# The seven block products of a feed-forward's up projection, in another order

## The chip, the core and the metric

The kernel runs on one core of a Trainium2 chip. The metric is the device time of one execution in microseconds (us); the time given for a kernel is the median of its runs. The kernel before takes 2684.95 us, the median of 3 runs (2684.22 to 2685.54).

The engines are named as the profile names them: PE is TensorE (matmuls), PEld its weight loads, DVE is VectorE, ACT is ScalarE, POOL is GpSimd, SP is SyncE, which only issues DMAs here. ACTq is ScalarE's queue as an issuer of DMAs. L250 is line 250 of the kernel.

## The reference

One decoder layer on x of 1024 rows and 1024 columns, all in float32: a SwiGLU feed-forward, a mixer (attention heads beside a state space scan), a cross-attention on 256 memory rows, and a second feed-forward, each with an RMS norm ahead of it and one behind it. The change touches only the first half of the two feed-forwards.

```python
D_MODEL = 1024; SEQ = 1024; D_FF = 2816
...
def swiglu(h, w_gu, w_down):
    gu = h @ w_gu
    g, u = jnp.split(gu, 2, axis=-1)
    return (jax.nn.silu(g) * u) @ w_down
...
    f = swiglu(rmsnorm(h, ffn1_pre_g[l]), ffn1_w_gu[l], ffn1_w_down[l])
    h = h + 0.5 * rmsnorm(f, ffn1_post_g[l])
...
    f = swiglu(rmsnorm(h, ffn2_pre_g[l]), ffn2_w_gu[l], ffn2_w_down[l])
    h = h + 0.5 * rmsnorm(f, ffn2_post_g[l])
```

## The kernel before, in words

**Numbers.** To keep float32 accuracy on TensorE, each operand is split into a high part (a cast on ScalarE, L248) and a low part (value minus high part, on VectorE, L250), both in the fp32r type. A product takes three matmuls for each slice of 128: high by high, high by low, low by high (mm3, L262). Activations lie transposed in tiles of 128 columns of the model by 512 rows (`XH`, `XL`, in the profile xh, xl), for two halves of the rows (hh = 0 and 1) and eight slices k.

**The up phase** (up_phase, L537) computes silu(g) times u for 22 blocks f of 128 columns of D_FF. For each f there are two weight blocks, G and U, and two halves of the rows: a 2 x 2 block product if the 1024 model columns are halved too. The first three f (PLAIN = 3) are done by plain projections, 96 matmuls each. While they run, the kernel prepares sums and differences of activation blocks, and from f = 3 on each f goes through `seven(f)` (L735), a scheme of seven block products in place of eight, 84 matmuls. B11 and B12 are the tiles of the first four slices of the two halves of rows, B21 and B22 those of the last four (L560). B21 and B12 are, by the time of the first seven, overwritten with differences (`steps` L647, `below` L662, `last` L670); S[1], S[4] and S[5] are sums in tiles of their own.

**The preparation** is driven by a list of events: `at(t, f)` (L675) puts an event at a time of a model clock that counts the matmuls issued so far; when the clock passes t the event's instructions are put into the program. `last(k)`, which writes B12's tiles, comes at the head of the first seven (L839 to L843); in feed-forward 1 `below(k)`, which writes B21's, comes in the last plain projections. Each such combination is one VectorE operation (L641), a cast on ScalarE and a subtraction on VectorE.

**The weights.** `pieces(f)` (L679) makes the seven weight blocks in the order in which the products want them: a sum or difference of quarters on GpSimd (L690) where the block is one, then the split (L248, L250) into a tile of a ring of 6 + NBLK (NBLK is 3 in feed-forward 1, 4 in feed-forward 2). `product` (L728) takes the oldest block and first makes sure that four are on their way (`ahead(4)`, L716). The raw G and U of block f + 1 are loaded when the first piece of block f is made.

**A seven** runs its products in the order B22, B21, S1, S4, B12, S5, B11. Each is 12 matmuls into a PSUM bank of 128 x 512 (`bank`, a ring of seven). Three banks are used twice: B12 accumulates on B22's bank a, S5 on S1's bank c, B11 on B21's bank b. Between the two uses the first content is read: a is copied to t5 by ScalarE (L742), b to d by ScalarE (L746), c is read by VectorE into e = d + c (L752), where d has become d - t5 on GpSimd (L747). Then e += m6 (L756); t1 = silu(a R) (L760); e += a (L762); t0 = silu((d + c) R) (L766, L767); t0 *= b (L770); e -= b (L772); t1 *= e on GpSimd (L773). R is the norm's factor of the row. t0 and t1 are stored by DMAs that ScalarE issues (L570), 4.5 us of the model clock later.

**Order of instructions.** TensorE's order is that of the program text. The other engines' order is set by a tile scheduler from dependences and priorities; the operations in `with self.urgent()` (L95) get a higher priority. The order within an engine is then fixed: an instruction that waits holds up everything behind it on its engine.

**What shares the up phase.** In feed-forward 1, `prepare` (L189) splits other weights of the layer beside the sevens, on ScalarE, VectorE and SP. In feed-forward 2, `act_sums` (L575) loads four stored blocks after every second f (GpSimd issues, L586), combines them on VectorE (L593), and ScalarE issues the stores of the sums (L598); the preparation's loads of x are issued by GpSimd (L625).

After the up phase comes the down projection: `down1` (L849) in feed-forward 1, `down_rows` in feed-forward 2. `down1` writes its operands over the tiles xh and xl.

Of the kernel before, what the change touches and what calls it, by code (L numbers as in the profile page):

```python
# [10 lines left out]
F32 = mybir.dt.float32  # L11
# [3 lines left out]
ALU = mybir.AluOpType  # L15
# [3 lines left out]
P = 128  # L19
S = 1024  # L20
H = 512
# [25 lines left out]
class Kern:  # L47
# [489 lines left out]
    def up_phase(self, sp, sp2, wgu, gpre, act_d, bank, load, plain, sizes, rw=None, begin=None):  # L537

        nc = self.nc
        NFT, NWC, NBLK = sizes  # L540

        fts, es = [self.t(sp, [P, H], F32, "ft", bufs=NFT)], [self.t(sp, [P, H], F32, "e")]

        def sums(dt):
            return {n: [self.t(sp, [P, 2, H], dt, f"S{n}{k}") for k in range(4)] for n in (1, 4, 5)}
# [12 lines left out]
        S = {n: [(x[:, 0], x[:, 1]) for x in v] for n, v in sums(F32R).items()}  # L558
        X = [[(self.XH[hh][k], self.XL[hh][k]) for k in range(KT)] for hh in range(2)]
        B11, B12, B21, B22 = X[0][0:4], X[1][0:4], X[0][4:8], X[1][4:8]  # L560

        def ft():
            return fts.pop() if fts else self.t(sp, [P, H], F32, "ft", bufs=NFT)
# [4 lines left out]
        def store(f, hh, t):  # L568
            o = act_d[f // 2][hh][:, f % 2, :]
            self.later.append((self.clock + 4500, lambda: self.kp(nc.scalar.dma_start(out=o, in_=t))))  # L570
            stored[f // 2] += 1
            if stored[f // 2] == 4 and not begin:
                act_sums(f // 2, self.clock + {0: 32000, 1: 26000}.get(f // 2, 10000))
# [36 lines left out]
        def scaled(t, src, hh):  # L610
            nc.vector.tensor_tensor(out=t, in0=src, in1=self.R[hh], op=ALU.mult)  # L611
            nc.scalar.activation(t, t, AF.Silu)  # L612
# [66 lines left out]
        def pieces(f):  # L679

            G, U = (load(wgu[2 * f + i], [P, KT, P]) for i in range(2))
            yield
            G0, G1, U0, U1 = G[:, 0:4], G[:, 4:8], U[:, 0:4], U[:, 4:8]
            for a, b, op in (
                (G0, G1, ALU.add), (U1, None, None), (G0, U1, ALU.add), (U0, G0, ALU.subtract), (G0, None, None),
                (G1, U1, ALU.subtract), (U0, U1, ALU.add),
            ):
                if b is not None:
                    t = self.t(sp if begin else sp2, [P, 4, P], F32, "wc", bufs=NWC)
                    nc.gpsimd.tensor_tensor(out=t, in0=a, in1=b, op=op)  # L690
                    a = t
                n = self.nblk = (self.nblk + 1) % (6 + NBLK)
                if n < 6:
                    w = self.t(self.wp, [P, 2, 4, P], F32R, ("whi", "wlo")[n % 2], bufs=3)
                else:
                    w = self.t(sp2, [P, 2, 4, P], F32R, "blk", bufs=NBLK)
                self.split(w[:, 0], w[:, 1], a)
                yield w

        def blocks():  # L700
            cur = pieces(PLAIN)
            next(cur)
            yield
            for f in range(PLAIN, NFF):
                nxt = None
                for i in range(7):
                    w = next(cur)
                    if i == 0 and f + 1 < NFF:
                        nxt = pieces(f + 1)
                        next(nxt)  # L710
                    yield w
                cur = nxt
# [11 lines left out]
        def block():  # L724
            ahead(4)
            return ready.pop(0)

        def product(ps, x, more=False):  # L728

            w = block()  # L730
            self.more = more
            self.mm3(ps, [(w[:, 0, k, :], w[:, 1, k, :], *x[k]) for k in range(4)], not more, True)
            self.more = False

        def seven(f):  # L735


            t5, d = (self.t(self.tp, [P, H], F32, f"sq{i}") for i in range(2))
            a = bank()
            product(a, B22)  # L740
            with self.urgent():
                nc.scalar.copy(t5, a)  # L742
            b = bank()
            product(b, B21)
            with self.urgent():
                nc.scalar.copy(d, b)  # L746
            nc.gpsimd.tensor_tensor(out=d, in0=d, in1=t5, op=ALU.subtract)  # L747
            c = bank()
            product(c, S[1])
            e = es.pop() if es else self.t(sp, [P, H], F32, "e")  # L750
            with self.urgent():
                nc.vector.tensor_tensor(out=e, in0=d, in1=c, op=ALU.add)  # L752
            m6 = bank()
            product(m6, S[4])
            with self.urgent():
                nc.vector.tensor_tensor(out=e, in0=e, in1=m6, op=ALU.add)  # L756
            product(a, B12, True)
            t1 = ft()
            with self.urgent():
                scaled(t1, a, 1)  # L760
            with self.urgent():
                nc.vector.tensor_tensor(out=e, in0=e, in1=a, op=ALU.add)  # L762
            product(c, S[5], True)
            t0 = ft()
            with self.urgent():
                nc.vector.tensor_tensor(out=t0, in0=d, in1=c, op=ALU.add)  # L766
            scaled(t0, t0, 0)  # L767
            product(b, B11, True)
            with self.urgent():
                nc.vector.tensor_tensor(out=t0, in0=t0, in1=b, op=ALU.mult)  # L770
            with self.urgent():
                nc.vector.tensor_tensor(out=e, in0=e, in1=b, op=ALU.subtract)  # L772
            nc.gpsimd.tensor_tensor(out=t1, in0=t1, in1=e, op=ALU.mult)  # L773
            store(f, 0, t0)
            store(f, 1, t1)
# [3 lines left out]
        t0, dt = (T0 + 12000, 7000) if begin else (T0 + 24000, 6500)  # L779
# [64 lines left out]
        for f in range(PLAIN, NFF):  # L844
            seven(f)
# [1492 lines left out]
```

## Time and profile before

| | before |
|---|---|
| median of 3 runs | 2684.95 us (2684.22 to 2685.54) |
| the profiled execution | 2688.81 us |
| its span | 2687.0 us |
| granted TensorE clock, mean over the span | 0.993 |
| idle time of PE by the page | 2687.0 - 2626.5 = 60.5 us |
| bytes moved | 477.75 MB, 178 GB/s in the mean |

How the rows of the prediction are read. The page's line of engines gives busy time, its share of the span and the number of instructions. The rows of the windows view begin with a stretch of the span and its length; then follows the busy time, with the number of instructions, of PE, PEld, DVE, ACT and POOL, then the mean granted TensorE clock, the busy share of the DMA engines, and GB/s. A row of the timeline gives the start of an instruction, its duration, the engine, the line, the operation, what it writes and reads with shapes, and xN if N alike ran on without a break; a bracket at the end is idle time of the engine just ahead of it and what ended that. Names of buffers are the program's: mm is a PSUM bank of the ring's first three, dn one of the other four, wraw and raw raw weights, wc a combined weight block, whi, wlo and blk split weight blocks, sq the tiles t5 and d, ft t0 and t1.

The groups that the change touches, in the page's numbers: GpSimd's weight combinations (L690) take 1433 to 1505 ns each where they run from raw tiles (114 of them, 167.4 us), the splits' casts (L248) 913 ns for a whole G or U of 128 x 1024, and the silu of a result (L612) 631 ns.

### The profile page before, as it was taken

The page shows a single profiled execution, that of the slowest core. Times are in us where ns is not written, and L with a number is a line of the kernel's source. Part 1 is how long each engine was busy: PE and PEld are TensorE (multiplying, and loading weights), DVE is VectorE, ACT ScalarE, POOL GpSimd, SP SyncE. Part 2 cuts the span into 40 slices and gives each one's busy share as a digit, 9 for nine tenths or more (in the row PEclk, how much of TensorE's full clock was granted, in tenths as well). Part 3 has the DMA queues.
Part 4 walks back from the last instruction along what each step waited for, and adds up shares of the span by engine and source line. Part 5 has one row for each costly group of instructions (what it writes and reads, how often), then busy time and mean ns, then how long its engine had stood idle before and what let it go on. Part 6 is the DMA issues. An engine that isn't in the chain of part 4 may idle for free.

```text
span 2687.0 us, 36694 instructions
## 1 busy us (share of the span) xinstructions
PE 2626.5 (98%) x12970; PEld 2179.5 (81%) x12970; DVE 1886.6 (70%) x2907; ACT 1272.3 (47%) x2263; POOL 605.0 (23%) x712
## 2 busy tenths in 40 slices
PE   9899999999999999999999999999999899999998
PEld 7788888888777778888888897887877788887787
DVE  7788887467568775677777877775557966566777
ACT  7444444445235563555555554354545333333553
POOL 2555553000100000111111110101013655552000
PEclk9999999999999999999999999999999999999999
DMA  5578888984532215544444465444357443447554
GB/s 211 186 266 283 277 287 274 341 290 156 205 125 79 79 67 189 142 107 108 119 119 124 152 193 206 173 141 149 110 181 270 161 162 132 147 140 277 166 169 149
DMA packets 204009, 477.75 MB, mean 178 GB/s; under 512 B 25009, under 2 KB 33585, under 8 KB 203825
## 3 DMA queue, kind: packets, MB, share of 16 engines
q1 hardware_dynamic: 157888, 366.59, 40.9%
q0 software_dynamic: 25344, 71.32, 8.8%
q10 hardware_dynamic: 20592, 37.50, 3.7%
q8 instruction: 102, 1.67, 0.3%
q14 instruction: 83, 0.67, 0.1%
HBM read 322.48 MB, written 131.86 MB: 169 GB/s over the span
## 4 chain that ended last, share of the span: by engine, by line
PE 80%; DMA 7%; DVE 7%; issue 3%; ACT 2%; POOL 0%; SPq 0%; DVEq 0%; ACTq 0%; POOLq 0%
PE mm L137 44%; PE dn L137 28%; PE z L137 2%; PE tr L140 2%; PE y L137 1%; PE ms L137 1%; PE ms L140 1%; DMA wraw<-act 1%; PE seg L137 1%; DMA oraw<-mix 1%; DVE wlo L250 1%; DMA wraw<-in_w_dn 1%; DMA dwlo<-bl 0%; DMA raw<-act 0%; PE st L137 0%
## 5 line engine op out<-in xcount | busy, mean ns | idle before, releaser
L137 PE MATMUL mm<-xh,whi 128*128 128x512 f32 x1364 | 537.2, 404 | 7.1 <-ACT xh L248 2.7
L137 PE MATMUL mm<-xh,wlo 128*128 128x512 f32 x1316 | 504.9, 393 | 0.6 <-ACT xh L248 0.6
L137 PE MATMUL mm<-xl,whi 128*128 128x512 f32 (+1 forms) x1258 | 490.5, 390 | 3.6 <-DVE xl L250 3.2
L137 PEld LDWEIGHTS mm<-xh,whi 128*128 128x128 f32 x1364 | 257.4, 189 | 52.8 <-issue 3.8
L137 PEld LDWEIGHTS mm<-xh,wlo 128*128 128x128 f32 x1316 | 247.9, 188 | 55.0 <-ACT xh L248 1.0
L137 PEld LDWEIGHTS mm<-xl,whi 128*128 128x128 f32 x1258 | 238.2, 189 | 39.1 <-DVE xl L250 4.6
L1734 DVE TENSOR_TENSOR_SCAN nb<-nb,begin 128x128 f32<-128x128 f32 (+7 forms) x128 | 171.8, 1353 | 57.9 <-ACT nb L1730 57.5
L1730 ACT ACTIVATE nb<-z,scale 128x128 f32<-128x128 f32 (+2 forms) x192 | 107.8, 580 | 80.6 <-PE z L137 80.3
L248 ACT CAST whi<-wraw 128x1024 fp32r<-128x1024 f32 (+1 forms) x102 | 93.1, 913 | 101.4 <-PE mm L137 63.5
L137 PE MATMUL dn<-xh,wlo 128*128 128x512 f32 x396 | 136.2, 391 | 1.5 <-DMA wlo<-dwlo 1.5
L250 DVE TENSOR_TENSOR wlo<-wraw,whi 128x1024 fp32r<-128x1024 f32 x70 | 85.4, 1221 | 55.4 <-ACT whi L248 55.0
L137 PE MATMUL dn<-xh,whi 128*128 128x512 f32 x356 | 122.8, 390 | 0.0
L1751 POOL DMA_DIRECT2D mix<-sq x64 | 52.8, 825 | 227.9 <-DVE sq L1749 166.8
L690 POOL TENSOR_TENSOR wc<-raw,wraw 128x512 f32<-128x512 f32 x56 | 84.3, 1505 | 74.6 <-issue 26.4
L690 POOL TENSOR_TENSOR wc<-wraw,raw 128x512 f32<-128x512 f32 x58 | 83.1, 1433 | 71.5 <-DVE blk L250 17.0
L612 ACT ACTIVATE ft<-ft 128x512 f32<-128x512 f32 x88 | 55.4, 631 | 76.3 <-DVE ft L611 75.8
L773 POOL TENSOR_TENSOR ft<-ft,e 128x512 f32<-128x512 f32 x38 | 62.2, 1637 | 129.0 <-DVE e L772 102.7
L250 DVE TENSOR_TENSOR atl<-tr,ath 128x512 fp32r<-128x512 f32 (+1 forms) x108 | 67.9, 632 | 32.1 <-ACT ath L248 31.6
L137 PE MATMUL dn<-xh,blk 128*128 128x512 f32 x280 | 90.3, 389 | 0.0
L137 PEld LDWEIGHTS dn<-xh,wlo 128*128 128x128 f32 x396 | 74.6, 188 | 17.7 <-DMA wlo<-dwlo 2.0
L137 PE MATMUL mm<-ath,v 128*128 128x256 f32 x320 | 86.0, 291 | 0.2 <-ACT ath L248 0.2
L250 DVE TENSOR_TENSOR whi<-wc,whi 128x512 fp32r<-128x512 f32 x80 | 64.7, 810 | 30.6 <-ACT whi L248 24.2
(542 smaller groups left out, 6614.8 us busy)
## 6 DMA issues: line engine op xcount, KB each, us to landing
whi<-dwhi SPq DMA_DIRECT2D x78, 512.0 KB, 3.3
wlo<-dwlo SPq DMA_DIRECT2D x78, 512.0 KB, 4.3
wraw<-in_w_gu SPq DMA_DIRECT2D x44, 512.0 KB, 4.1
act<-ft ACTq DMA_DIRECT2D x88, 256.0 KB, 2.5
raw<-in_w_gu SPq DMA_DIRECT2D x38, 512.0 KB, 4.4
h<-F POOLq DMA_DIRECT2D x40, 256.0 KB, 3.0
xl<-h POOLq DMA_DIRECT2D x40, 256.0 KB, 5.7
dwhi<-acc SPq DMA_DIRECT2D x39, 256.0 KB, 5.1
```

The costliest lines, as they stand in the source:

```text
L137: self._pe(self.nc.tensor.matmul(out, lhsT, rhs, start=start, stop=stop, skip_group_check=self.more), cost)
L140: self._pe(self.nc.tensor.transpose(out, src, self.ident if ident is None else ident), 109.0)
L248: self.kp(self.nc.scalar.copy(hi, src))
L250: self.nc.vector.tensor_tensor(out=lo, in0=src, in1=hi.bitcast(F32), op=ALU.subtract)
L612: nc.scalar.activation(t, t, AF.Silu)
L690: nc.gpsimd.tensor_tensor(out=t, in0=a, in1=b, op=op)
L773: nc.gpsimd.tensor_tensor(out=t1, in0=t1, in1=e, op=ALU.mult)
L1730: nc.scalar.activation(nb[:, s0:s1], z[:, 0:n], AF.Sigmoid, scale=sc[:, i : i + 1])
L1734: nc.vector.tensor_tensor_scan(out=nb[:, 0:Wd][:, ::-1], data0=nb[:, 0:Wd][:, ::-1], data1=begin[:, S - Wd : S][:, ::-1], initial=0.0, op0 ...
L1751: nc.gpsimd.dma_start(out=self.mix_d[p][a * 64 : a * 64 + 64, csl], in_=o, accum_op=ALU.add)
```

## The change

The seven products of `seven(f)` run in the order B22, S1, S4, B21, S5, B11, B12. The weight pieces (L684) are made in the order that goes with it. The banks' pairs are the same: S5 on S1's, B11 on B21's, B12 on B22's. Since d does not exist yet when S1 is done, S1's bank is copied to e by ScalarE, S4's is added to e by VectorE, and d is added to e by VectorE after S5. The last product of a seven is now B12, whose bank gives t1 by scaling and silu; B11 is the last but one. In the changed kernel's own line numbers S1's copy to e is L747, e += m6 L751, B21's copy to d L755, GpSimd's d - t5 L756, t0 = d + c L760, e += d L763, B11's t0 *= b L766 and e -= b L768, B12's e += a L774 and the GpSimd product L775; behind `seven` all lines are higher by two.

```diff
--- before.py
+++ after.py
@@ -682,8 +682,8 @@
             yield
             G0, G1, U0, U1 = G[:, 0:4], G[:, 4:8], U[:, 0:4], U[:, 4:8]
             for a, b, op in (
-                (G0, G1, ALU.add), (U1, None, None), (G0, U1, ALU.add), (U0, G0, ALU.subtract), (G0, None, None),
-                (G1, U1, ALU.subtract), (U0, U1, ALU.add),
+                (G0, G1, ALU.add), (G0, U1, ALU.add), (U0, G0, ALU.subtract), (U1, None, None), (G1, U1, ALU.subtract),
+                (U0, U1, ALU.add), (G0, None, None),
             ):
                 if b is not None:
                     t = self.t(sp if begin else sp2, [P, 4, P], F32, "wc", bufs=NWC)
@@ -740,36 +740,38 @@
             product(a, B22)
             with self.urgent():
                 nc.scalar.copy(t5, a)
+            c = bank()
+            product(c, S[1])
+            e = es.pop() if es else self.t(sp, [P, H], F32, "e")
+            with self.urgent():
+                nc.scalar.copy(e, c)
+            m6 = bank()
+            product(m6, S[4])
+            with self.urgent():
+                nc.vector.tensor_tensor(out=e, in0=e, in1=m6, op=ALU.add)
             b = bank()
             product(b, B21)
             with self.urgent():
                 nc.scalar.copy(d, b)
             nc.gpsimd.tensor_tensor(out=d, in0=d, in1=t5, op=ALU.subtract)
-            c = bank()
-            product(c, S[1])
-            e = es.pop() if es else self.t(sp, [P, H], F32, "e")
+            product(c, S[5], True)
+            t0 = ft()
             with self.urgent():
-                nc.vector.tensor_tensor(out=e, in0=d, in1=c, op=ALU.add)
-            m6 = bank()
-            product(m6, S[4])
+                nc.vector.tensor_tensor(out=t0, in0=d, in1=c, op=ALU.add)
+            scaled(t0, t0, 0)
             with self.urgent():
-                nc.vector.tensor_tensor(out=e, in0=e, in1=m6, op=ALU.add)
+                nc.vector.tensor_tensor(out=e, in0=e, in1=d, op=ALU.add)
+            product(b, B11, True)
+            with self.urgent():
+                nc.vector.tensor_tensor(out=t0, in0=t0, in1=b, op=ALU.mult)
+            with self.urgent():
+                nc.vector.tensor_tensor(out=e, in0=e, in1=b, op=ALU.subtract)
             product(a, B12, True)
             t1 = ft()
             with self.urgent():
                 scaled(t1, a, 1)
             with self.urgent():
                 nc.vector.tensor_tensor(out=e, in0=e, in1=a, op=ALU.add)
-            product(c, S[5], True)
-            t0 = ft()
-            with self.urgent():
-                nc.vector.tensor_tensor(out=t0, in0=d, in1=c, op=ALU.add)
-            scaled(t0, t0, 0)
-            product(b, B11, True)
-            with self.urgent():
-                nc.vector.tensor_tensor(out=t0, in0=t0, in1=b, op=ALU.mult)
-            with self.urgent():
-                nc.vector.tensor_tensor(out=e, in0=e, in1=b, op=ALU.subtract)
             nc.gpsimd.tensor_tensor(out=t1, in0=t1, in1=e, op=ALU.mult)
             store(f, 0, t0)
             store(f, 1, t1)
```

## The prediction

> **What bounds the kernel now.** I read the page first, then the busy time by windows, TensorE's rows in order of time where the windows show gaps, and last the other engines' rows around those gaps.
>
> ```profile
> span 2687.0 us, 36694 instructions
> PE 2626.5 (98%) x12970; PEld 2179.5 (81%) x12970; DVE 1886.6 (70%) x2907; ACT 1272.3 (47%) x2263; POOL 605.0 (23%) x712
> 80.00:105.00 25.00, 18.15 (x65) 13.21 (x64) 23.55 (x25) 15.08 (x26) 16.81 (x17) 0.88 0.48 171
> 105.00:200.00 95.00, 95.00 (x412) 78.41 (x411) 75.62 (x96) 43.20 (x76) 57.06 (x36) 0.98 0.72 244
> 2068.00:2122.00 54.00, 43.72 (x175) 33.50 (x174) 47.11 (x52) 24.40 (x42) 35.87 (x32) 0.95 0.45 151
> 2122.00:2300.00 178.00, 178.00 (x778) 147.20 (x777) 123.77 (x169) 58.94 (x102) 101.04 (x87) 0.99 0.44 153
> 302.45 19.04 PE dn L137 x84
> ```
>
> TensorE is busy 98%. Inside the seven-product loops it is busy 95.00 of 95.00 us and 178.00 of 178.00 us: there the order of products can save nothing, it can only break something. One seven (84 matmuls) takes 19.04 us, a product 2.72 us, a matmul 2.72 / 12 = 0.227 us. TensorE is idle at the head of each feed-forward's loop: 18.15 of 25 us with VectorE busy 23.55, and 43.72 of 54 with VectorE busy 47.11. TensorE's rows there:
>
> ```profile
> 80.15 0.39 PE L137 MATMUL mm<-xh,whi 128*128 128x512 f32 x1
> ...
> 87.55 0.50 PE L137 MATMUL mm<-xl,wlo 128*128 128x512 f32 x1 [2.93 <-DVE xl L250]
> ...
> 101.22 0.50 PE L137 MATMUL mm<-xh,whi 128*128 128x512 f32 x1 [2.10 <-ACT xh L248]
> 102.96 0.80 PE L137 MATMUL mm<-xl,whi 128*128 128x512 f32 x1 [1.24 <-DVE xl L250]
> ...
> 103.98 5.30 PE L137 MATMUL dn<-S,wlo 128*128 128x512 f32 x12
> ...
> 111.89 0.39 PE L137 MATMUL dn<-xh,blk 128*128 128x512 f32 x1
> ```
>
> ```profile
> 2074.37 0.50 PE L137 MATMUL mm<-xh,whi 128*128 128x512 f32 x1 [0.45 <-ACT whi L248]
> ...
> 2082.62 0.73 PE L137 MATMUL dn<-S,whi 128*128 128x512 f32 x2 [1.19 <-ACT whi L248]
> ...
> 2094.68 0.50 PE L137 MATMUL mm<-xl,whi 128*128 128x512 f32 x1 [1.13 <-DVE xl L250]
> 2102.33 0.39 PE L137 MATMUL dn<-xh,blk 128*128 128x512 f32 x1
> ...
> 2120.48 5.49 PE L137 MATMUL mm<-S,whi 128*128 128x512 f32 x12 [4.39 <-DVE e L752]
> ...
> 2128.81 0.39 PE L137 MATMUL mm<-xh,whi 128*128 128x512 f32 x1
> ```
>
> The first seven of feed-forward 1 runs from 80.15 to 111.89, 31.74 us: 12.7 lost, waiting for B21's and B12's operands (xh, xl) and then running S5 at half pace. Feed-forward 2's first seven (2074.37 to 2102.33) loses 8.9; its second (to 2128.81) loses 7.4, because S5 accumulates into S1's bank and VectorE reads that bank late (e L752). So 29.0 us, 1.1%, is all there is to win.
>
> **The change part by part.** *Matmuls* are the same 84 per seven; banks and their ring of seven are the same.
>
> *Later use of B21 and B12.* B21 goes from second to fourth, B12 from fifth to seventh: 5.44 us more for each.
>
> ```profile
> 88.84 0.69 DVE L250 TENSOR_TENSOR xl<-bh,xh 128x512 fp32r<-128x512 f32 x1 [0.68 <-ACT xh L248]
> ...
> 101.20 1.71 DVE L250 TENSOR_TENSOR xl<-bh,xh 128x512 fp32r<-128x512 f32 x1
> ```
>
> In feed-forward 1, B21's last operand is ready at 89.53. TensorE would ask for it at 80.15 + 3 x 2.72 + 9 x 0.227 = 90.35: no wait. B12's last comes at 102.91; asked for at 98.5 if nothing else waits, later if something does.
>
> *A new reader, on ScalarE.* S1's bank was read by VectorE (e = d + c, L752). Now ScalarE copies it to e; S5 is fifth, so it must wait for that copy. In the built program's order this copy stands where the copy of B21's bank (L746) stood, behind a cast of B12's operand and a block's cast:
>
> ```profile
> 94.67 0.62 ACT L248 CAST xh<-bh 128x512 fp32r<-128x512 f32 x1 [0.30 <-DVE bh L641]
> 95.20 0.62 ACT L248 CAST blk<-wc 128x512 fp32r<-128x512 f32 x1
> 95.72 0.58 ACT L746 COPY sq<-mm 128x512 f32<-128x512 f32 x1
> ```
>
> So it ends near 96.3, held by VectorE's chain, not by TensorE. TensorE reaches S5 at 80.15 + 4 x 2.72 = 91.03: a wait of 5.3 us. After the idle time at 98.7 to 103 and before 2120.48, twelve matmuls took 5.30 and 5.49 us, so I take S5 at half pace: 96.3 + 5.3 = 101.6. B11 then needs ScalarE's copy of B21's bank (L755 of the changed kernel), which stands behind the casts of two blocks of the next seven; the second needs a GpSimd combination that in the trace starts at 100.70:
>
> ```profile
> 100.70 1.65 POOL L690 TENSOR_TENSOR wc<-wraw,raw 128x512 f32<-128x512 f32 x1 [1.23 <-DVE blk L250]
> ```
>
> Taking about 99.5 for it there (the GpSimd subtraction ahead of it moves away), copy done 102.4, then B11 and B12: 102.4 + 5.44 = 107.9 against 111.89. **Gain 4.0**; bounds 0 (the copies 4 us later) and 12.7.
>
> The Trainium skill ("TensorE: Matmul & The Clock Gate", Part 1) says the clock halves only after an idle window of about 3.4 us. The trace agrees at 2120.48 (4.39 us idle) but at 101.22 and 102.96 single gaps of 2.10 and 1.24 us, one matmul between them, sufficed. By the page's rule taken gap by gap, the 2.5 us wait that I expect below ahead of B11 would stay at full pace, and the sum would be 10.4 instead of 8.4.
>
> *Feed-forward 2, first seven.* Block 1 is now a combination, and GpSimd makes it ahead of eight DMA issues:
>
> ```profile
> 2073.62 4.25 POOL L625 DMA_DIRECT2D blk<-h  x8
> 2081.46 0.58 ACT L746 COPY sq<-mm 128x512 f32<-128x512 f32 x1 [2.13 <-PE mm L137]
> 2081.94 0.62 ACT L248 CAST whi<-wc 128x512 fp32r<-128x512 f32 x1
> ```
>
> Those loads start 1.3 us later. Block 2's cast stands behind ScalarE's copy of the second product's bank, as it does now (81.46, then 81.94, and TensorE idle 1.19 + 0.66): S4 loses about 2.0. B12's waits go, but block 5's split stands behind VectorE's new e + d, which waits for GpSimd's d - t5, which waits for B21's copy: I put B11's wait at 2.5 to 3.8 us, half pace after it 2 us. Lost: 1.5 (first product, unchanged) + 2.0 + 3.0 + 2.0 = 8.5 against 8.9. **Gain 0.4**; bounds 0 less 3 and 7.4.
>
> *Feed-forward 2, second seven.* VectorE's late read is gone; ScalarE's copy stands behind two DMA issues of the activations' sums (L598) that wait for VectorE:
>
> ```profile
> 2112.41 0.33 ACTq L598 DMA_DIRECT2D xs<-xl  x1
> 2114.71 0.33 ACTq L598 DMA_DIRECT2D xs<-xl  x1
> 2114.00 0.68 DVE L593 TENSOR_TENSOR xl<-cb,cb 128x512 f32<-128x512 f32 x1
> 2119.75 0.68 DVE L752 TENSOR_TENSOR e<-sq,mm 128x512 f32<-128x512 f32 x1
> ```
>
> By these rows the copy is possible at 2115.0, 4.7 us before VectorE's read today; S5 would be asked for near 2102 + 10.9 = 2112.9. That costs a wait of 0 to 2.2 plus part of the half pace; I take 3.4 lost of today's 7.4. **Gain 4.0**; bounds 0 and 7.4.
>
> *Steady sevens.* ScalarE gets 38 copies of 0.58 us: 22 us beside its 47%; cover is there. The cover of B21's bank falls from four products between its copy and B11 to one, 2.72 us. SP: G's raw tile is released by piece 6 instead of 4, so the load two sevens ahead starts some 5 us later, of a whole seven's cover: 0. Ends: feed-forward 1's down projection writes its operands over B12's tiles, free 5.44 us later; they are wanted 4 steps of 5.44 us into that stage, and are cast now at 454.31, where the seven ends at 111.89 + 18 x 19.04 = 454.6: 0. Feed-forward 2's end goes through scale, silu and one GpSimd product instead of two VectorE operations and the same product: 0.1. If those covers fail it costs what rival 3 says.
>
> **Sum:** 4.0 + 0.4 + 4.0 = 8.4. The profiled execution (2688.81 around a span of 2687.0) lies 3.9 above the median; against itself it would go to 2680.4, and the median to 2684.95 - 8.4 = 2676.6.
>
> **Rivals.** (1) *The copies come in time*: VectorE, relieved of waiting for products, runs ahead and none of the three stalls remains but the first product's 1.5: 29.0 - 1.5 = 27.5 less, 2657.5. For it: 2119.75 is late only by VectorE's backlog. Against: VectorE busy 23.55 of 25.
>
> (2) *The stall only changes its name*: S5 and B11 wait as long as B12 did; 2684.95, between 2680 and 2690. For it: VectorE, the engine that is late, loses no instruction.
>
> (3) *Slower: the one-product cover fails in every other seven of feed-forward 2.* There ScalarE's copy of B21's bank stands behind three DMA issues that wait for VectorE's sums, and these for a load:
>
> ```profile
> 2230.04 0.55 POOL L586 DMA_DIRECT2D dg<-act  x1 [0.81 <-DMA act<-ft]
> 2232.84 1.46 DVE L593 TENSOR_TENSOR xl<-cb,cb 128x512 f32<-128x512 f32 x2 [3.02 <-DMA cb<-act]
> 2228.66 0.56 POOL L586 DMA_DIRECT2D cb<-act  x1
> 2347.83 1.29 DVE L593 TENSOR_TENSOR xl<-cb,cb 128x512 f32<-128x512 f32 x2 [3.93 <-DMA cb<-act]
> ```
>
> The load from 2228.66 was used at 2232.84, 4.2 us; so dg is there at 2234.2, two sums 2235.5, the issues and the copy 2236.6. That seven starts at 2128.81 + 5 x 19.04 = 2224.0 and asks for B11 at 2237.6: 1.0 us to spare. At 2347.83 the load came 0.75 us later in its seven. From 1 us of lateness on it costs; 2.2 us in each of 8 sevens is 18 us: 2676.6 + 18 = 2694.6.
>
> **How the numbers follow.** Forecast (gain 5.4 to 16): 0.50. Rival 1 (more than 16): 0.12. Rival 2: 0.25. Rival 3: 0.13. A measurement of this kernel tells about 0.2%, 5.4 us, from no change. So faster 0.62, same 0.25, slower 0.13. The likeliest is 2676.6. The range goes from part of rival 1 (2664) to the end of rival 2 (2690); rival 3 and the best of rival 1 lie outside. The forecast's own range is 2669 to 2680.
>
> **What would show it.** Right: in feed-forward 1's first seven no wait on xl or xh in B21, a wait of about 5 us ahead of S5 (dn or mm<-S) put down to ScalarE's new copy, and the second seven starting near 107.9; the wait on e in feed-forward 2's second seven gone or below 2.5 us; TensorE without gaps in 2122 to 2440. Wrong: gaps ahead of B11 in every other seven (rival 3), or the heads' lost time unchanged (rival 2), or S5 started without a wait (rival 1).

## The result and the profile after

The changed kernel takes 2698.06 us (median of 7 runs, 2695.74 to 2699.64), the kernel before 2685.54 (7 runs, 2684.22 to 2692.53): a ratio of 1.0042, 95% interval 1.0032 to 1.0052. It is slower by about 0.4%, where 2676.6 was forecast. The profiled execution took 2699.64 around a span of 2697.9.

The first lines of the page and two stretches of the windows view (columns as before) of the kernel after:

```profile
span 2697.9 us, 36779 instructions
PE 2627.8 (97%) x12970; PEld 2178.1 (81%) x12970; DVE 1885.7 (70%) x2907; ACT 1287.7 (48%) x2301; POOL 605.1 (22%) x712
140.00:460.00 320.00, 317.00 (x1386) 260.65 (x1385) 259.77 (x336) 155.99 (x283) 165.43 (x108) 0.99 0.81 274
2130.00:2470.00 340.00, 331.34 (x1445) 271.30 (x1444) 216.84 (x308) 115.87 (x204) 179.09 (x146) 0.99 0.44 155
```

TensorE's busy time is 1.3 us more and its idle time 70.1 us instead of 60.5: of the 10.9 us by which the span is longer, 9.6 are idle. And idle time lies where there was none: in the steady sevens, 3.0 us of 320 and 8.7 of 340. TensorE's own rows of the kernel after name what it waited for (not all of them are shown):

```profile
96.38 5.41 PE L137 MATMUL mm<-S,whi 128*128 128x512 f32 x12 [5.47 <-ACT e L747]
102.36 0.50 PE L137 MATMUL dn<-xh,wlo 128*128 128x512 f32 x1 [0.57 <-ACT sq L755]
...
220.97 0.75 PE L137 MATMUL mm<-xh,whi 128*128 128x512 f32 x1 [2.17 <-ACT sq L755]
...
2126.59 0.50 PE L137 MATMUL mm<-xh,whi 128*128 128x512 f32 x1 [2.62 <-ACT sq L755]
...
2147.41 0.50 PE L137 MATMUL dn<-xh,blk 128*128 128x512 f32 x1 [1.46 <-ACT sq L755]
2169.88 0.66 PE L137 MATMUL mm<-xh,blk 128*128 128x512 f32 x1 [3.11 <-ACT sq L755]
...
2327.72 0.50 PE L137 MATMUL dn<-xh,whi 128*128 128x512 f32 x1 [1.86 <-ACT sq L755]
```

The first row is the head that was forecast: S5 waits for S1's copy and then runs at half pace. All the other rows shown are one thing: B11, the first matmul into B21's bank after ScalarE's copy L755. In feed-forward 2 they come in the second and third seven, and from the fourth on in every other. S1's copy (L747) makes three shorter waits that are not shown: 0.26 and 0.49 us in feed-forward 1's second and seventh seven, 1.64 in feed-forward 2's second.

To compare kernels I cut each trace at the sevens. A seven starts 2.72 us (new order) or 5.44 us (old order) ahead of its first matmul on S1; feed-forward 2's first is taken from its first matmul (2074.37 in before, 2079.50 in after), since it has a gap within the first product. A is the start of feed-forward 1's second seven, B the time lost in the 17 from there to the start of its last (over 17 x 19.04), C the length of feed-forward 2's first two sevens, D the time lost in the 16 from its third to the start of its last (over 16 x 19.04), E the rest, so that A + 323.68 + B + C + 304.64 + D + E is the span.

| kernel (run) | A | B | C | D | E | span | median |
|---|---|---|---|---|---|---|---|
| before | 111.89 | 0.0 | 54.4 | 0.0 | 1892.4 | 2687.0 | 2685.5 |
| before, second trace (e0) | 110.48 | 0.0 | 53.3 | 1.0 | 1890.1 | 2683.2 | |
| after | 107.93 | 6.6 | 52.7 | 13.0 | 1889.4 | 2697.9 | 2698.1 |
| d on VectorE (e1) | 108.35 | 0.2 | 53.8 | 6.6 | 1886.1 | 2683.3 | 2687.1 |
| B12, then B11 (e2) | 106.14 | 4.1 | 49.6 | 4.1 | 1889.9 | 2682.1 | 2684.7 |
| sums stored by SyncE (e3) | 106.15 | 6.6 | 48.3 | 14.8 | 1889.1 | 2693.2 | 2694.9 |
| old order, S1 copied by ScalarE (e4) | 107.58 | 6.9 | 51.8 | 1.3 | 1903.1 | 2699.0 | 2700.5 |
| the same by VectorE (e4 vector) | 109.99 | 5.4 | 53.2 | 2.7 | 1896.9 | 2696.6 | 2700.2 |
| first two sevens new (e5) | 107.31 | 1.7 | 51.5 | 5.8 | 1889.8 | 2684.5 | 2687.7 |
| e1 and sums 5 us later (e6) | 108.45 | 0.2 | 55.0 | 1.3 | 1887.6 | 2680.8 | 2685.7 |
| e2's order in the heads alone (e8) | 106.09 | 1.6 | 48.5 | 8.9 | 1889.8 | 2683.1 | 2687.9 |
| e1 and e2 together (e7) | 105.55 | 1.6 | 48.8 | 0.1 | 1888.4 | 2672.7 | 2674.3 |
| e7, S1 copied by VectorE | 107.25 | 1.5 | 48.3 | 4.1 | 1885.7 | 2675.2 | 2683.4 |
| old order, d on VectorE (e9) | 109.51 | 0.0 | 51.5 | 0.1 | 1893.8 | 2683.3 | 2682.8 |

Runs of one kernel spread by 1 to 15 us here, and one trace is one execution: the two traces of before differ by 1.0 to 2.3 us in A, C, D and E each. Differences of that size are not read. The ratios below are to the kernel before, run beside each kernel (medians 2685.66 to 2686.5).

### The profile page after: what moved, and what is told of

Read it like the earlier page. It is cut to its first block, busy times and chain, and to the rows that moved or that the text cites. A ratio compares the mean times of both kernels' runs of the same rounds, so it can differ in the third digit from the quotient of the medians.

```text
span 2697.9 us, 36779 instructions
## 1 busy us (share of the span) xinstructions
PE 2627.8 (97%) x12970; PEld 2178.1 (81%) x12970; DVE 1885.7 (70%) x2907; ACT 1287.7 (48%) x2301; POOL 605.1 (22%) x712
## 4 chain that ended last, share of the span: by engine, by line
PE 69%; DVE 7%; DMA 5%; issue 4%; ACT 2%; POOL 1%; SPq 0%; ACTq 0%; DVEq 0%; POOLq 0%
PE mm L137 38%; PE dn L137 22%; PE z L137 2%; PE tr L140 2%; PE y L137 1%; PE ms L137 1%; PE ms L140 1%; PE seg L137 1%; DMA act<-ft 1%; DMA raw<-act 1%; DVE whi L250 1%; DVE wlo L250 1%; POOL wc L690 1%; DMA oraw<-mix 0%; PE st L137 0%
## 5 line engine op out<-in xcount | busy, mean ns | idle before, releaser
L248 ACT CAST ath<-tr 128x512 fp32r<-128x512 f32 (+1 forms) x108 | 58.9, 546 | 57.4 <-PE tr L140 52.5
L137 PE MATMUL mm<-atl,v 128*128 128x256 f32 x320 | 83.0, 282 | 0.7 <-DVE atl L250 0.7
```

The source lines that it names most:

```text
L137: self._pe(self.nc.tensor.matmul(out, lhsT, rhs, start=start, stop=stop, skip_group_check=self.more), cost)
L248: self.kp(self.nc.scalar.copy(hi, src))
```

## Where the copy was late

One such chain, feed-forward 2's gap at 2327.72, from the rows of GpSimd, VectorE and ScalarE (kernel after). The seven at hand starts at 2312.10:

```profile
2304.51 0.59 ACT L755 COPY sq<-mm 128x512 f32<-128x512 f32 x1
```

```profile
2304.97 1.28 POOL L690 TENSOR_TENSOR wc<-wraw,raw 128x512 f32<-128x512 f32 x1 [0.33 <-DVE wlo L250]
2306.95 1.60 POOL L690 TENSOR_TENSOR wc<-raw,wraw 128x512 f32<-128x512 f32 x1 [0.70 <-DVE whi L250]
2308.52 1.28 POOL L756 TENSOR_TENSOR sq<-sq,sq 128x512 f32<-128x512 f32 x1
```

```profile
2309.83 0.69 DVE L763 TENSOR_TENSOR e<-e,sq 128x512 f32<-128x512 f32 x1 [2.43 <-POOL sq L756]
...
2315.43 0.68 DVE L774 TENSOR_TENSOR e<-e,dn 128x512 f32<-128x512 f32 x1
```

```profile
2316.86 1.30 POOL L775 TENSOR_TENSOR ft<-ft,e 128x512 f32<-128x512 f32 x1
2320.73 0.56 POOL L586 DMA_DIRECT2D dg<-act  x1 [1.32 <-DMA act<-ft]
```

```profile
2325.39 1.29 DVE L593 TENSOR_TENSOR cb<-cb,dg 128x512 f32<-128x512 f32 x2 [3.14 <-issue]
```

```profile
2318.19 0.33 ACTq L570 DMA_DIRECT2D act<-ft  x1
...
2326.11 0.93 ACTq L598 DMA_DIRECT2D xs<-cb  x2
2327.08 0.59 ACT L755 COPY sq<-dn 128x512 f32<-128x512 f32 x1 [5.02 <-DVE cb L593]
```

In the seven before, B21's bank was copied by 2305.10, but GpSimd makes d = d - t5 only behind two weight combinations; VectorE stands 2.43 us for it, and t0's and t1's operations stand behind that. So t1 is finished late, ScalarE issues its store at 2318.19, the load of dg, which waits for that store, is issued at 2320.73, 8.63 us into the seven, VectorE's sums (L593) wait for dg until 2325.39 (this row names no releaser; the row of the same operation in e1, below, names the load), ScalarE's stores of the sums (L598) wait for VectorE, and L755 stands behind them. B11 asked for the bank at 2312.10 + 5 x 2.72 = 2325.7.

The later this load, the longer the seven. In feed-forward 2's even sevens from the fourth to the fourteenth, dg is issued 9.95, 6.84, 7.03, 6.72, 8.63 and 7.60 us into the seven, and the seven is 5.0, 0.5, 0.9, 0.4, 2.2 and 1.1 us too long (in the sixteenth and eighteenth 6.8 into it, and 0.4 and 0.7 too long); in the trace of before the same six loads are issued at 7.07, 6.54, 6.03, 5.84, 5.87 and 5.96.

In feed-forward 1's longest such gap (220.97) L755 stands behind a cast of the background split (L209), whose target is still being stored:

```profile
219.81 0.62 ACT L209 CAST rpost<-braw 128x512 fp32r<-128x512 f32 x1 [1.54 <-DMA dwhi<-rpost]
220.33 0.58 ACT L755 COPY sq<-mm 128x512 f32<-128x512 f32 x1
```

## The experiments

**e1: d made by VectorE.**

```diff
-            with self.urgent():
-                nc.scalar.copy(d, b)
-            nc.gpsimd.tensor_tensor(out=d, in0=d, in1=t5, op=ALU.subtract)
+            with self.urgent():
+                nc.vector.tensor_tensor(out=d, in0=b, in1=t5, op=ALU.subtract)
```

> Change after, with one part replaced: d = b - t5 is made by one VectorE operation that reads B21's bank, in place of ScalarE's copy (L755) and GpSimd's subtraction (L756). Theory Q (ScalarE's queue: the copy L755 stands in order behind instructions that wait, the casts of the background split L209 in feed-forward 1 and the issues L598 of the sums in feed-forward 2, and S5's 2.72 us is all its cover): feed-forward 1's 6.6 us of lost time after its first seven go, of feed-forward 2's 13.0 at least half, since VectorE's sums still wait for the same load: 2698.1 - 6.6 - 6.5 to 13 = 2678 to 2685. Theory D (the root is d itself: GpSimd makes it late, VectorE stands waiting for it, so t0, t1, t1's store and the load that the sums wait for all come late): the same in feed-forward 1, and in feed-forward 2 the load of dg is issued about 3 us earlier in its seven and nearly all of the 13.0 goes: 2678 to 2680. Rival L (not the queue, but the 38 more copies on ScalarE and the weight blocks' other order cost the time): the copies of S1's bank and the blocks' order are still there, so 2692 to 2698.

Measured: 2687.1, ratio to before 1.0005 (0.9996 to 1.0014). B fell from 6.6 to 0.2, D from 13.0 to 6.6: all of feed-forward 1, half of feed-forward 2. The load of dg is issued 5.8 us into its seven (2149.71, the seven from 2143.92) instead of 6.7 to 10: theory D is right in that. But VectorE still stands for that load, and now d itself stands behind it:

```profile
2154.70 1.29 DVE L593 TENSOR_TENSOR cb<-cb,dg 128x512 f32<-128x512 f32 x2 [3.25 <-DMA dg<-act]
...
2157.72 0.68 DVE L755 TENSOR_TENSOR sq<-mm,sq 128x512 f32<-128x512 f32 x1
```

```profile
2158.45 0.50 PE L137 MATMUL mm<-xh,blk 128*128 128x512 f32 x1 [0.78 <-DVE sq L755]
```

So theory Q's half stands too. Rival L (the extra copies themselves cost; the next expectation has its price) falls for the steady sevens: the copies of S1 and the blocks' order were all there. The median lies 2 us above Q's range, further above D's. Since e1 takes a copy off ScalarE and an operation off GpSimd at once, it does not say which of the two made feed-forward 1's loss.

**e2: B12 ahead of B11**, the last two weight pieces exchanged with them: two products of cover for B21's copy instead of one.

```diff
-                (U0, U1, ALU.add), (G0, None, None),
+                (G0, None, None), (U0, U1, ALU.add),
...
-            product(b, B11, True)
...
             product(a, B12, True)
...
+            product(b, B11, True)
```

> Change after, with its last two products exchanged (S5, B12, B11, and the last two weight pieces with them): B21's copy has two products, 5.44 us, before B11 asks for the bank. Theory Q: the longest wait was 3.1 us, so the steady gaps go: 2698.1 - 6.6 - 13.0 = 2678.5; in feed-forward 1's first seven B12 is asked for at 101.8, about 1 us before its last operand is there, so 2679.5; 2677 to 2683. Theory D: the copy's wait is covered all the same, as in Q, but t0 and e still come late and so do the store and the load: the wait on ScalarE may grow beyond 3.1, 2680 to 2686. Rival L: as many copies as before, 2695 to 2700.

Measured: 2684.66, ratio 1.0000 (0.9990 to 1.0009). From feed-forward 1's third seven and feed-forward 2's fifth on no seven is longer than 19.04. What stays lies near the heads: S1's copy in feed-forward 1's second seven (all of B), and B21's copy, above all, in feed-forward 2's fourth:

```profile
119.54 4.41 PE L137 MATMUL dn<-S,whi 128*128 128x512 f32 x12 [2.36 <-ACT e L747]
...
2162.16 0.50 PE L137 MATMUL mm<-xh,blk 128*128 128x512 f32 x1 [2.36 <-ACT sq L755]
```

The extra copies alone, then, do not make the steady loss: e2 has them all. That the second product of cover is the cure is shown only in part, because e2 moves the dates too (ScalarE's rows in e2, one of feed-forward 1 and one of feed-forward 2):

```profile
216.47 0.59 ACT L755 COPY sq<-mm 128x512 f32<-128x512 f32 x1 [0.73 <-PE mm L137]
...
2235.91 0.59 ACT L755 COPY sq<-dn 128x512 f32<-128x512 f32 x1 [3.70 <-DVE cb L593]
```

In feed-forward 1 the copy now waits for its own product alone and ends 11.7 us into each seven from the third on (after: up to 16.7), where even the changed kernel would ask for the bank only at 5 x 2.72 = 13.6. It is no longer late there, and the runs do not say which part of the new order did that. In feed-forward 2 the load of dg is issued 5.8 us into five of the eight even sevens (after: 6.7 to 10), but the copy still stands behind VectorE's sums, and from the sixth seven on ends up to 14.3 us in: there the second product hides up to 0.7 us.

The total is 1.7 us above theory Q's range, by the waits near the heads, and inside theory D's; but D's late load is there mainly in one seven, feed-forward 2's fourth (11.7 us into it).

**e3: the sums' stores (L598) issued by SyncE.**

```diff
-                self.kp(nc.scalar.dma_start(out=xs_d[n, j], in_=x.pop(n)))
+                self.kp(nc.sync.dma_start(out=xs_d[n, j], in_=x.pop(n)))
```

> Change after, with the stores of the activations' sums in feed-forward 2 (L598) issued by SyncE instead of ScalarE: nothing on ScalarE ahead of L755 waits for VectorE's sums any more. Theory Q: the gaps ahead of B11 in feed-forward 2 go (up to 13.0 us), feed-forward 1 keeps its 6.6: 2698.1 - 11 to 13 = 2685 to 2687. Theory D: the lateness of d is untouched, L755 comes in time and TensorE does not see it: the same 2685 to 2687, with the load of dg as late in its seven as now (about 9 us); it differs from Q only in what it leaves in the rows. Rival L: 2695 to 2700.

Measured: 2694.94, ratio 1.0038 (1.0026 to 1.0051). Both theories' 2685 to 2687 missed, and the time lies at the edge of rival L's range: D did not fall, it is 14.8. Feed-forward 1 kept its 6.6, and dg is issued 8.8 to 11.2 us into its seven, as theory D had it. In feed-forward 2's steady sevens the wait at B11 is gone and has moved to S5, which waits for S1's copy; ahead of that ScalarE stands at the store of t1:

```profile
2177.90 0.50 PE L137 MATMUL dn<-xh,wlo 128*128 128x512 f32 x1 [1.34 <-DVE e L774]
2182.01 3.06 PE L137 MATMUL dn<-S,whi 128*128 128x512 f32 x12 [1.10 <-ACT e L747]
```

```profile
2179.94 0.33 ACTq L570 DMA_DIRECT2D act<-ft  x1
2180.36 0.59 ACT L742 COPY sq<-dn 128x512 f32<-128x512 f32 x1 [2.45 <-POOL ft L775]
...
2181.37 0.59 ACT L747 COPY e<-dn 128x512 f32<-128x512 f32 x1
```

The seven started at 2168.24, so t1's store comes 11.7 us into it; VectorE's part of the seven before (L774, for which B21's bank waits too) is as late. Taking one waiting instruction out of ScalarE's queue left the lateness, and the next one held the queue.

**e4: old order, S1's bank copied by ScalarE and d added to e after S5** (one part of the change alone), **and the same with the copy on VectorE.**

```diff
-                nc.vector.tensor_tensor(out=e, in0=d, in1=c, op=ALU.add)
+                nc.scalar.copy(e, c)        # second run: nc.vector.tensor_copy(e, c)
...
             scaled(t0, t0, 0)
+            with self.urgent():
+                nc.vector.tensor_tensor(out=e, in0=e, in1=d, op=ALU.add)
```

> Kernel before in its old order of products and weight blocks, with one part of the change alone: S1's bank is copied to e by ScalarE and d is added to e by VectorE after S5, 38 more ScalarE copies of 0.58 us. Theories Q and D: the copy of B21's bank keeps its four products of cover, S1's copy has two, nothing in the steady sevens is late: 2685.5 less up to 4 (the wait of 4.4 us on e in feed-forward 2's second seven goes), 2681 to 2687. Rival L: the copies cost as in the change, 2691 to 2698.

> As the run with the old order and S1's bank copied to e (2700.5), with the copy on VectorE instead of ScalarE: as many instructions more, none on ScalarE. If ScalarE's queue made the 15 us (the copy behind casts of the background split that wait for stores), they go: 2685.7 plus or minus 3. If the extra operations themselves or the later end of e (d added after S5) made them: 2693 to 2701.

Measured: 2700.5, ratio 1.0056 (1.0043 to 1.0069), and 2700.19, ratio 1.0052 (1.0039 to 1.0065). Theories Q and D failed, and rival L came nearest (2.5 us above its range): this small part alone costs 15 us in the old order. It is not that S1's copy stands in ScalarE's queue, since the copy on VectorE costs as much; whether the extra operations or the later end of e make it, the two runs do not separate. It is lost in feed-forward 1 (B 6.9 and 5.4) and behind it (E), where the down projection waits for ScalarE's copies of its own banks (L945): 7.4 us in e4, 4.1 in the second run, 0.5 in before. The longest of e4's:

```profile
480.01 0.50 PE L137 MATMUL mm<-xh,whi 128*128 128x512 f32 x1 [2.66 <-ACT F L945]
```

The windows view of 140 to 430, first before, then e4 (the fifth number is VectorE's busy time):

```profile
140.00:430.00 290.00, 290.00 (x1281) 240.15 (x1280) 238.33 (x302) 135.22 (x238) 170.91 (x107) 1.00 0.82 277
```

```profile
140.00:430.00 290.00, 287.47 (x1251) 232.92 (x1250) 256.73 (x294) 133.86 (x245) 170.77 (x104) 1.00 0.80 270
```

VectorE works 18 us more with 8 operations fewer: 0.87 us each instead of 0.79. In e1 it is 225.02 us with 318, 0.71 each, and GpSimd has 138.69 us instead of 170.91:

```profile
140.00:430.00 290.00, 290.00 (x1281) 240.11 (x1280) 225.02 (x318) 135.51 (x240) 138.69 (x90) 1.00 0.84 280
```

In feed-forward 1 VectorE had little slack, and what it has depends on how its operations fall beside GpSimd's. That e4's loss comes from this is argued from these rows and not shown; no run took GpSimd's operations away in e4.

**e5: the new order in the first two sevens of each feed-forward alone; e8: e2's order in feed-forward 1's first and feed-forward 2's first two.** `seven_old` is the function before, and the pieces' order is chosen likewise.

```diff
-            seven(f)
+            seven(f) if f < PLAIN + 2 else seven_old(f)    # e8: PLAIN + (1 if begin else 2)
```

> The change's order of products and weight blocks only in the first two sevens of each feed-forward, the order before in the other 17. If the heads' gain and the steady loss are separate things, the heads keep what the change's trace shows against that of before (feed-forward 1's second seven starts 3.96 us earlier but lasts 0.56 longer, feed-forward 2's first lasts 0.8 longer, its second 2.5 shorter: 5.1 us in all), and the sevens behind them run at 19.04 us: 2685.7 - 5.1 = 2680.6, 2677 to 2684. If instead the steady loss comes from work that the new heads leave behind (the stores, loads and sums shifted for good), gaps go on behind the second seven: 2685 to 2692.

> New order B22, S1, S4, B21, S5, B12, B11 in the first seven of feed-forward 1 and the first two of feed-forward 2 only, the order before in all others. From the trace with that order throughout: feed-forward 1's second seven starts 5.75 us earlier than before, feed-forward 2's first seven lasts 0.6 shorter and its second 4.25 shorter, 10.6 in all: 2685.7 - 10.6 = 2675, if the first sevens of the old order behind them run at 19.04 us; with one more half-pace stall of 4 us at each seam 2683.

Measured: 2687.73, ratio 1.0004 (0.9995 to 1.0012), and 2687.91, ratio 1.0009 (1.0000 to 1.0018). Feed-forward 1's head keeps its gain (A), less 1.6 to 1.7 us in the sevens behind it (B). Feed-forward 2's does not: what its first two sevens win, the third gives back and more (C and D; e5, the first seven of the old order):

```profile
2143.29 4.34 PE L137 MATMUL dn<-S,blk 128*128 128x512 f32 x12 [3.94 <-DVE e L799]
```

That is VectorE's late read of S1's bank, the same that kernel before has one seven earlier. TensorE had run ahead of VectorE; the wait was only put off. Neither forecast came: e5 lies in its second range, but by one late seven and not by gaps that go on, and e8 is 5 us above the 2683 that it was given with a stall at each seam.

**e6: e1, with the sums and their stores recorded 5 us later.**

```diff
-                at(t0 + 9000 + 1200 * i, combine, n, out, a, b, op)
-                at(t0 + 12000 + 1200 * i, put, n)
+                at(t0 + 14000 + 1200 * i, combine, n, out, a, b, op)
+                at(t0 + 17000 + 1200 * i, put, n)
```

> As the run in which VectorE makes d = b - t5 (2687.1), and beside it the activations' sums of feed-forward 2 and their stores (L593, L598) are recorded 5 us later on the model clock, so that the load which they wait for is there. There the rest of the loss was 0.45 to 0.78 us ahead of B11 in every other seven, VectorE standing 3.2 us for the load of dg with d behind it. Theory (in-order engines held by that load): these gaps go, 6.5 us, 2680.6, 2678 to 2684. Rival (the gaps are the price of d itself on VectorE, or of the sums' own work): they stay, 2686 to 2688.

Measured: 2685.67, ratio 1.0000 (0.9991 to 1.0009), between the two ranges. The gaps in every other seven are gone (D 1.3, all of it in the third and fourth seven): the wait for the load made them. The total followed only in part: of the 5.3 us that D lost against e1, 1.2 came back in C and 1.5 in E, and the profiled run is the fastest of its kernel, 3.1 us below the median. In feed-forward 2's second seven d now came later still (6.17 us, 3.57 in e1):

```profile
2117.12 0.79 PE L137 MATMUL mm<-xh,whi 128*128 128x512 f32 x1 [6.17 <-DVE sq L755]
```

**e7: both cures**, the edits of e1 and e2; **and S1's bank copied by VectorE too** (`nc.vector.tensor_copy(e, c)`).

> Order B22, S1, S4, B21, S5, B12, B11 and d = b - t5 by one VectorE operation: the two cures together. Each alone left, by its trace, 6.5 us (d on VectorE, B11 before B12) and 4.1 us (B12 before B11) in feed-forward 2's steady sevens, and 4.05 in feed-forward 1's second seven (S1's copy late). If what is late is d and the copy of B21's bank, all steady gaps go and the second seven's stays: 2685.7 - 10.6 (heads) + 4 = 2679, 2675 to 2683. If VectorE's own standing for the sums' load holds S5's operands or the blocks instead: 2683 to 2688.

> As e7_both, with S1's bank copied to e by VectorE instead of ScalarE: no bank of the new order but B22's is read by ScalarE. If ScalarE's queue makes S1's copy late in the heads, their waits ahead of S5 (3.4 to 5.5 us in feed-forward 1's first seven) shrink by 2 us or more and the time is 1 to 5 us below that of e7_both. If VectorE's backlog is what sets the heads (busy 23.55 of 25 us there), the copy waits there as long: the same, or up to 4 us more than e7_both.

Measured: 2674.32, ratio 0.9955 (0.9942 to 0.9969), and 2683.44, ratio 0.9991 (0.9980 to 1.0002). e7 is 0.7 us below its forecast range and faster than both kernels, by 12 us than before (0.45%) and by about 24 than after, which ran in an earlier round. Steady gaps are gone (D 0.1), the heads keep most of their gain. Three of the waits that are left in feed-forward 1 and in feed-forward 2's second seven:

```profile
95.33 4.60 PE L137 MATMUL mm<-S,whi 128*128 128x512 f32 x12 [4.35 <-ACT e L747]
...
117.90 3.02 PE L137 MATMUL dn<-S,whi 128*128 128x512 f32 x12 [1.31 <-ACT e L747]
...
2113.37 0.50 PE L137 MATMUL mm<-xh,wlo 128*128 128x512 f32 x1 [2.45 <-DVE sq L755]
```

With S1's copy on VectorE too, the head's wait is no shorter (4.96 us at 96.44) and feed-forward 2's third seven loses 4.1: ScalarE's queue is not what makes S1's copy late in the heads. That VectorE's backlog does is the reading that is left, but it allowed 4 us more than e7, not 9. The trace is of the fastest of the runs (2677.0) and shows only 2.5 of the 9 us.

**e9: old order, with the edit of e1; e0: the kernel before once more.**

> Old order of products and weight blocks, with d = b - t5 made by one VectorE operation instead of ScalarE's copy and GpSimd's subtraction. Theory V (VectorE is what the sevens lean on, and its operations take 1.2 to 1.8 us instead of 0.68 while GpSimd combines): one GpSimd operation of 1.3 to 1.75 us less in each seven takes 10 to 15 us off VectorE's busy time in 290 us of feed-forward 1 (238 before), steady sevens stay at 19.04, the heads lose 2 to 8 us less than their 29: 2678 to 2684. Rival: VectorE gets 38 operations more and is the late engine in the heads: 2685 to 2690.

> The kernel before once more, for a second trace of it: all other traces here need 247 to 250.5 us from the start of feed-forward 2's last seven to the end, that of before 253.55. If the difference lies in the execution and not in the kernel, this one is at 247 to 251 too; if it belongs to the kernel, it stays near 253.5, and the new orders gain about 4 us behind the last seven that the forecast did not have.

Measured: 2682.8, ratio 0.9981 (0.9969 to 0.9994): d on VectorE alone is worth 0.2%, within theory V's range. VectorE is busy 232.15 us between 140 and 430 instead of 238.33, 6 less where V said 10 to 15. A and C are below both traces of before, by 1.0 to 2.9 us, hardly more than those two differ, so that the gain lies in the heads is not shown. In e0, feed-forward 2's last seven starts 250.8 us ahead of the end (before 253.55, after 248.1): half of the gain behind the last seven that a comparison of the first two traces shows belongs to the execution, as far as one more trace can tell.

## Why the prediction was wrong

**The sum.** 8.4 us less was forecast, 12.5 more came. By the two traces the heads won 4.0 (A) and 1.7 (C), the steady sevens lost 6.6 (B) and 13.0 (D), and 3.0 were won outside them (E): 10.9 more. The 3.0 were in no forecast, and 2.3 of them stand in the second trace of before too.

**Feed-forward 1's head: right.** S1's copy was to end near 96.3 and S5 to run 5.3 us at half pace: S5 started at 96.38 and took 5.41. The second seven was to start at 107.9: 107.93. Against the second trace of before the gain is 2.6, not 4.0; and the second seven itself lost 0.6, which the forecast did not have.

**Feed-forward 2's first seven:** 0.4 less was forecast, 0.8 more came (28.74 against 27.96). Its terms were near (first product 2.1 for 1.5, B11's waits 3.8 together for 2.5 to 3.8).

**Its second:** 4.0 less was forecast, 2.5 came. S5's wait was within its bounds (1.64 of 0 to 2.2). Not seen was B11's wait of 2.62 in the same seven. Against the second trace of before (24.23) nothing is left of the gain.

**Steady sevens: the step that failed.** "The cover of B21's bank falls from four products between its copy and B11 to one, 2.72 us", at a cost of 0. It cost 6.6 + 13.0 = 19.6 us, nearly all of it at B11 behind that copy and in the half pace after it, more than the heads could give. The mechanism stood in the text as rival 3, with 0.13 and a margin of 1.0 us. Its sum was good: with dg issued 6.03 us into the seven 1.0 us is to spare, so lateness begins at 7.0, and in the trace after a load at 6.7 already costs 0.4. What was wrong is the date, taken from the one row of before at 2230.04; the same trace has 7.07 and 6.54 in the fourth and sixth seven. The load waits for t1's store, and t1's work had moved: it is behind the last product, and behind a d that is now made in the second half of the seven. It came 6.7 to 10 us into the seven. The step on feed-forward 2's end looked at the new last operations and put them at 0.1 us; it did not ask what stands ahead of them on VectorE. For feed-forward 2 the runs bear this out: with d made early (e1) the load is back at 5.8 and half of D goes, and with VectorE's wait for the load taken away as well (e6) most of the rest does.

**Feed-forward 1's share was in no rival.** Cover was said to be there because ScalarE was busy 47%. Busy time was the wrong number: ScalarE's queue stands for stores and for other engines (1.54 us ahead of the cast at 219.81), and an instruction behind those is late on an idle engine. Why the same cast and copy come in time in e2, with two products of cover that they do not need there, stays open.

**Rival 2** (the stall changes its name) came true in feed-forward 2's head: C is 52.7 against 54.4 and 53.3, with waits at S5 and B11 in place of the one for e. **Rival 1** did not come about.

## What to carry to other kernels

A read that frees a bank needs cover for everything that may stand ahead of it in its engine's queue: look at the longest wait in that queue, not at the engine's busy share. Whoever moves work must move the dates of all that waits for its result, the DMA that reads back a stored tile too, before a margin of 1 us is taken from an old trace. When a stall goes away by letting TensorE run ahead of a backlogged engine, look for it in the next iteration; here it went where the engines also had less to do (e7, with d made in one operation).

## What the runs showed of the hardware that was not expected

**Equal gaps, unequal clocks.** The rows give the granted clock (the number behind GpSimd's) in about 3 us behind a gap of TensorE. Kernel after, gaps of 2.17, 3.11 and 2.62 us:

```profile
220.97:223.97 3.00, 3.00 (x7) 2.42 (x8) 1.33 (x2) 1.60 (x3) 3.00 (x3) 0.51 1.06 381
2169.88:2172.90 3.02, 3.02 (x8) 2.37 (x9) 2.45 (x3) 1.08 (x2) 2.72 (x2) 0.53 0.44 165
2126.59:2129.59 3.00, 3.00 (x13) 2.49 (x14) 1.75 (x2) 0.99 (x2) 2.15 (x3) 1.00 0.94 364
```

Kernel e2, both behind 2.36 us:

```profile
119.54:122.20 2.66, 2.66 (x6) 2.15 (x7) 2.16 (x3) 2.66 (x6) 1.08 (x1) 0.50 0.29 105
2162.16:2164.90 2.74, 2.74 (x12) 2.24 (x13) 2.41 (x4) 1.08 (x2) 2.03 (x2) 1.00 0.83 254
```

The same gap halved the clock once and left it whole once, so between about 2 and 3 us the length of a gap does not decide. The Trainium skill ("TensorE: Matmul & The Clock Gate", Part 1) says that activity is watched in windows that run freely, not from the kernel's start; that fits equal gaps with unequal ends. Its condition of a whole idle window of about 3.4 us does not fit: the gap of 2.17 us is shorter than that.

**One operation, two durations.** Between 140 and 430 us of the kernel after, e += d takes 1.62 us in the mean. It starts there as GpSimd's subtraction ends, and in most of these sevens GpSimd goes on with a combination just ahead of it (GpSimd's row, then VectorE's):

```profile
145.27 1.29 POOL L690 TENSOR_TENSOR wc<-wraw,raw 128x512 f32<-128x512 f32 x1
```

```profile
145.34 1.77 DVE L763 TENSOR_TENSOR e<-e,sq 128x512 f32<-128x512 f32 x1 [1.17 <-POOL sq L756]
```

In e1 VectorE's operation comes first. It takes 0.68 us, and the combination that starts 0.15 us behind it is the longer one (VectorE's row, then GpSimd's):

```profile
141.50 0.68 DVE L762 TENSOR_TENSOR e<-e,sq 128x512 f32<-128x512 f32 x1
```

```profile
141.65 1.68 POOL L690 TENSOR_TENSOR wc<-wraw,raw 128x512 f32<-128x512 f32 x1 [0.63 <-DVE blk L250]
```

The Trainium skill ("SBUF — State Buffer", SBUF: two separate sides) says that a VectorE operation with two inputs in SBUF and a GpSimd operation that reads SBUF exclude each other for a whole instruction. The rows agree: the one that starts first takes its short time (1.29 us for GpSimd's, 0.68 for VectorE's), and the one behind it takes longer than its own by 1.09 us (VectorE's) or 0.39 (GpSimd's). At 2309.83, where no combination follows GpSimd's subtraction at once, the same operation takes 0.69 us.
